# A decoder block on one Trainium2 core: the first projection pair in a written order on three engines, with x loaded ahead of the weights

## The chip, the cores and the metric

One core of one Trainium2 chip. The metric is device time in microseconds (us) of one execution; the kernel before has a median of 2082.65 us in three runs (2078.64 to 2083.49).

## What is computed

A decoder layer on 512 tokens of width 2048, all in float32. The reference, cut to what matters:

```python
h = rms_norm(x, norm1_g)
proj = h @ w_in                       # 2048 x 6160, split into eight parts
qa, ka, va, ra, ga, qb, kb, vb = split(proj)
log_g = log_sigmoid(ga @ gla_gate_w2 + gla_gate_b) / 16
out_a = gla_mixer(qa, ka, va, ra, log_g, gla_onorm_g)      # 4 heads, chunks of 64
out_b = dilated_mixer(norm(qb), norm(kb), vb, rel_bias)    # 8 heads
x = x + concat(out_a, out_b) @ w_out
h2 = rms_norm(x, norm2_g)
x = x + (silu(h2 @ w_gate) * (h2 @ w_up)) @ w_down
```

## The kernel before

**Pairs.** Every matrix product is done in pairs of 512 output columns (`pair`, L183 to L284). One pair multiplies 512 tokens by two neighbouring blocks of 512 columns, by a scheme of the Strassen-Winograd kind: seven products (P1 to P7) of sums of quarters in place of eight plain ones. In the pairs of the projection a product is a sum over four groups g, so a pair has 7 x 4 = 28 steps. A step takes one weight tile of 256 x 512 (called a, b, c or d by its quarter, or a difference of two of these, formed on VectorE at L238, L241, L246 or L251), and splits it into a high part, cast to the short TensorE format on ACT (`wh`, L253), and a low part, the remainder, on VectorE (`wl`, L255). Then TensorE does 12 matmuls of 128 x 128 by 128 x 512 (L263): eight with the high part and four with the low part. The token side is split in the same way beforehand (`Operand.split`, L129 on ACT and L130 on VectorE): operands A11, A12, A22 and the sums S1 to S4, seven for each group, each 128 x 512 in both parts.

**The first pair** (columns 0 to 1023, giving qa and ka) begins with nothing in memory. x has to be loaded, transposed on TensorE block by block (`x_turn`, L422: four transposes of 128 x 128 into one PSUM bank), and scaled by the norm's gain on the way out of PSUM (L429 on VectorE, or L434 on ACT in two halves). The squares of x are summed on ACT (`x_norm`, L407), and four small POOL operations (L411, L113, L114, L415) turn a sum into the row scale `rs1`, which is applied when an accumulator is copied out: the "seed" (L201, ACT), which a later product completes in "close" (L213, VectorE).

**Order.** The program is written as a pair's steps with `step()` between them, which takes the next pieces from a list `background`; `startup()` is the first of them and prepares the operands. A scheduler then orders the instructions on each engine by its own costs. Loads are all issued by SP, in order; at most eight are in flight, and load n waits for load n - 8. `LOADS` gives their order at the start: the gains of the norms, then x in eight pieces of 128 rows x 1024 columns (512 KB) mixed with the weight tiles.

**The gates.** The second pair's steps carry the work of `gates()`: 64 matmuls of 128 x 256 (`ranks`, L505) multiply the operands A11, A12, A22 and S1 by the 16 columns of w_in for the gate, whose small load is `gaw` (L375; tile k), rearranged by three POOL operations (L515 to L517) and split into `gs` (L524, L525). Then come the gate matmuls and the attention heads, in the steps of this pair and the next ones.

**Memory around it.** PSUM has four accumulator buffers (`acc`) and four banks (`bank`). `wh` and `wl` have two buffers each, the weight tiles twelve.

Of the kernel before, what the change touches and what calls it, by code (L numbers as in the profile page):

```python
# [18 lines left out]
P = 128  # L19
# [43 lines left out]
def block_kernel(ctx: ExitStack, tc: tile.TileContext, ins, out):  # L63
# [15 lines left out]

    uid = [0]  # L80

    def nm(s):
        uid[0] += 1
        return f"{s}_{uid[0]}"
# [19 lines left out]
    load(mats, ins["mats"])  # L104
# [74 lines left out]
    def pair(op, rows, w1, w2, final, step, seed_scale=None, pre=()):  # L179
# [3 lines left out]
        q = dict(pre)  # L183
# [102 lines left out]

    background = []
# [68 lines left out]
    def g1_load():  # L356
        load(grow[:, 0, :], ins["norm1_g"].rearrange("(k p) -> k p", p=P))
        load(grow[:, 1, :], ins["norm2_g"].rearrange("(k p) -> k p", p=P))
# [7 lines left out]
    def x_load(t, c):  # L366
        xt[t, c] = apool.tile([P, 1024], F32, name=nm("x"), tag="A")
        load(xt[t, c], x[t * P : (t + 1) * P, c * 1024 : (c + 1) * 1024])
# [30 lines left out]
    ss1 = const([P, 8], "ss1")  # L399
# [3 lines left out]
    raw = {}  # L403

    def x_norm(t):
        for c in range(2):
            tc.keep_in_program_order(nc.scalar.activation(  # L407
                work("L", bufs=2).bitcast(mybir.dt.bfloat16), xt[t, c], AF.Square,
                accum_out=ss1[:, 2 * t + c : 2 * t + c + 1],
            ))  # L410
        nc.gpsimd.tensor_tensor(  # L411
            rs1[:, t : t + 1], ss1[:, 2 * t : 2 * t + 1], ss1[:, 2 * t + 1 : 2 * t + 2], op=ALU.add
        )
        rsqrt_mean(rs1[:, t : t + 1], rs1[:, t : t + 1], D)
        nc.gpsimd.tensor_scalar(nrs1[:, t : t + 1], rs1[:, t : t + 1], -1.0, None, op0=ALU.mult)  # L415

    def x_turn(h, b):
        bk = bank().rearrange("p (j n) -> p j n", j=2)
        for jj in range(2):
            k = 2 * b + jj  # L420
            for m in range(2):
                nc.tensor.transpose(  # L422
                    bk[:, jj, m * P : (m + 1) * P],
                    xt[2 * h + m, k // 8][:, (k % 8) * P : (k % 8 + 1) * P],
                    ident,
                )
        dst = raw[b, h]
        if h == 0 and (b // 2 + b) % 2 == 0:
# [12 lines left out]
    builders = []  # L441
    pre = {}
    for what in LOADS.split():
        if what[0] == "x":
            x_load(int(what[1]), int(what[2]))
        elif what == "g":
            g1_load()
        else:
            pre[what[0], int(what[1])] = load_quarter(
                rows_in, what[0], int(what[1]), col({"a": 0, "b": 512, "d": 512}[what[0]])  # L450
            )

    def first_half(g):
# [7 lines left out]
        x_turn(0, 2 * g)  # L461
        t, b = 2 * g, 2 * g + 1
        builders.append(opx.build(g, raw[t, 0], raw[t, 1], raw[b, 0], raw[b, 1]))
        next(builders[g])

    for g in range(4):
        first_half(g)
    ls_d = [dram([P, 512], f"ls_d{t}") for t in range(4)]

    def startup():  # L470
        small_loads()
        for b in range(8):
            x_turn(1, b)
            yield
        for g, b in enumerate(builders):
            next(b)
            next(b)
            x_norm(g)
            yield
        for b in range(1, 8, 2):  # L480
            x_turn(0, b)
            yield
        for _ in range(2):
            for b in builders:
                next(b)
                yield
        for b in builders:
            yield from b

    def gates():  # L490
        gp = bank()

        def ranks(half):


            parts = (("A22", 2), ("S1", 0)) if half else (("A11", 0), ("A12", 1))
            dst = gp[:, half * 256 : half * 256 + 256]
            n = 0
            for name, kind in parts:
                for g in range(4):  # L500
                    a = opx.t[name, g]
                    for jj in range(2):
                        i = 8 * kind + 2 * g + jj
                        for hl in range(2):
                            nc.tensor.matmul(  # L505
                                dst,
                                gsplit[i // 12][:, i % 12 * 32 : i % 12 * 32 + P],
                                a[:, jj, hl, :],
                                start=(n == 0), stop=(n == 31),
                            )  # L510
                            n += 1
# [7 lines left out]
        gsplit = [mp.tile([P, 512], F32R, name=nm("gs"), tag=t, bufs=1) for t in ("q", "qT")]  # L519
        for i, t in enumerate(gsplit):  # L520
# [6 lines left out]
            )  # L527
        w2 = work("PT")
# [4 lines left out]
        yield  # L533
        ranks(1)
        yield
        ranks(0)
        yield
        ga = work("k", (32, 512))
        nc.scalar.copy(ga, gp[:32, :])
# [7 lines left out]
        )  # L547
        yield
# [687 lines left out]
```

## Time and profile before

| | |
|---|---|
| median of 3 runs | 2082.65 us (2078.64 to 2083.49) |
| profiled execution, time | 2082.12 us |
| its span, first to last instruction | 2079.9 us |
| TensorE busy | 2034.0 us, 98% |
| VectorE busy | 1664.6 us, 80% |
| ACT busy | 1103.5 us, 53% |
| granted TensorE clock, mean | 0.995 |
| moved by DMA | 358.30 MB, 172 GB/s |

In the profile PE is TensorE's matmul queue, PEld its weight loads, DVE VectorE, POOL GpSimd, SP the queue that issues the DMAs. Lines such as L263 are lines of the kernel before. In the timeline the columns are start, duration, engine, line, operation, output <- inputs with the shape, and in brackets the idle time of the engine before it and what ended it. In the waits they are: who waited, for whom, total us, times, longest. PE's duration of one matmul contains the way through the array; matmuls follow each other faster than that.

### The profile page before, as it was taken

Reading aid. Unit: us, or ns where it says so; the run is one execution under the profiler, and the core shown is the slowest. Engines: PE = TensorE matmul, PEld = TensorE weight load, DVE = VectorE, ACT = ScalarE, POOL = GpSimd, SP = SyncE. Lnnn points to the kernel's source line nnn. Section 1 sums busy time; section 2 is a strip of 40 time slices with the busy share of each in tenths; the row PEclk is TensorE's granted clock in tenths of the full one; section 3 lists DMA queues with packets and bytes.
Section 4 is the critical chain, followed back from the end, with each engine's and each line's share of the span. In section 5 each row is a group of like instructions: output and inputs, shape, how many; then the busy total and the mean of one; then the engine's idle time right before and its main releaser. Section 6 shows DMA issues by size and latency. Waiting matters only on the chain.

```text
span 2079.9 us, 25964 instructions
## 1 busy us (share of the span) xinstructions
PE 2034.0 (98%) x9290; PEld 1664.3 (80%) x9290; DVE 1664.6 (80%) x1849; ACT 1103.5 (53%) x1582; POOL 72.0 (3%) x108
## 2 busy tenths in 40 slices
PE   6899999999998999999999999999999999999999
PEld 4688777788876787888888888888888888888887
DVE  5976778677789888878778778778779989979977
ACT  5644455456676676445445445445446645545443
POOL 1100121002000000000000000000000000000000
PEclk9999999999999999999999999999999999999999
DMA  6334572736474866544544543543545855845762
GB/s 221 107 111 159 183 213 76 222 92 208 127 253 139 267 221 195 176 152 133 171 152 133 165 153 129 164 153 129 164 152 156 290 173 186 308 158 181 244 202 72
DMA packets 232683, 358.30 MB, mean 172 GB/s; under 512 B 18039, under 2 KB 92352, under 8 KB 232553
## 3 DMA queue, kind: packets, MB, share of 16 engines
q1 hardware_dynamic: 232552, 356.64, 53.7%
q8 instruction: 73, 1.20, 0.2%
q14 instruction: 58, 0.47, 0.1%
HBM read 294.43 MB, written 64.51 MB: 173 GB/s over the span
## 4 chain that ended last, share of the span: by engine, by line
PE 88%; DMA 4%; DVE 4%; ACT 1%; issue 1%; SPq 1%; POOL 0%; DVEq 0%; ACTq 0%
PE acc L263 82%; PE bank L830 1%; DVE wl L255 1%; PE bank L715 1%; PE bank L737 1%; DVE AS L130 1%; DMA k<-y_d 1%; DMA x<-in_x 1%; ACT wh L253 1%; DMA xn_d<-oT 0%; PE bank L730 0%; PE bank L656 0%; PE bank L638 0%; DMA r<-xn_d 0%; PE bank L505 0%
## 5 line engine op out<-in xcount | busy, mean ns | idle before, releaser
L263 PE MATMUL acc<-wh,AS 128*128 128x512 f32 x3136 | 789.0, 393 | 14.8 <-ACT AS L129 10.6
L263 PEld LDWEIGHTS acc<-wh,AS 128*128 128x128 f32 x3136 | 587.0, 189 | 147.3 <-ACT AS L129 12.7
L253 ACT CAST wh<-wa 128x1024 fp32r<-128x1024 f32 x392 | 412.4, 1054 | 456.6 <-PE acc L263 413.2
L263 PE MATMUL acc<-wh,AA 128*128 128x512 f32 x2352 | 590.2, 393 | 1.2 <-ACT wh L253 1.2
L255 DVE TENSOR_TENSOR wl<-wa,wh 128x1024 fp32r<-128x1024 f32 x392 | 478.1, 1221 | 128.9 <-ACT wh L253 123.1
L263 PEld LDWEIGHTS acc<-wh,AA 128*128 128x128 f32 x2352 | 439.2, 189 | 93.9 <-ACT wh L253 2.1
L263 PE MATMUL acc<-wl,AS 128*128 128x512 f32 x1568 | 421.8, 391 | 4.0 <-DVE wl L255 3.9
L263 PEld LDWEIGHTS acc<-wl,AS 128*128 128x128 f32 x1568 | 294.9, 188 | 67.9 <-DVE wl L255 6.3
L263 PE MATMUL acc<-wl,AA 128*128 128x512 f32 x1176 | 315.3, 390 | 1.0 <-DVE wl L255 1.0
L263 PEld LDWEIGHTS acc<-wl,AA 128*128 128x128 f32 x1176 | 220.4, 188 | 48.4 <-DVE wl L255 2.6
L253 ACT CAST wh<-wb 128x1024 fp32r<-128x1024 f32 x98 | 103.2, 1053 | 137.3 <-PE acc L263 132.2
L253 ACT CAST wh<-wc 128x1024 fp32r<-128x1024 f32 x98 | 103.1, 1053 | 131.7 <-PE acc L263 123.4
L253 ACT CAST wh<-wd 128x1024 fp32r<-128x1024 f32 x98 | 103.3, 1054 | 114.0 <-PE acc L263 103.4
L255 DVE TENSOR_TENSOR wl<-wc,wh 128x1024 fp32r<-128x1024 f32 x98 | 119.6, 1222 | 54.3 <-ACT wh L253 53.9
L255 DVE TENSOR_TENSOR wl<-wd,wh 128x1024 fp32r<-128x1024 f32 x98 | 119.6, 1222 | 54.1 <-ACT wh L253 54.0
L251 DVE TENSOR_TENSOR wa<-wc,wa 128x1024 f32<-128x1024 f32 x98 | 119.6, 1223 | 38.4 <-DMA wc<-in_w_gate 23.0
L255 DVE TENSOR_TENSOR wl<-wb,wh 128x1024 fp32r<-128x1024 f32 x98 | 119.3, 1220 | 12.1 <-ACT wh L253 12.0
L246 DVE TENSOR_TENSOR wb<-wd,wb 128x1024 f32<-128x1024 f32 x98 | 119.6, 1221 | 0.5
L241 DVE TENSOR_TENSOR wa<-wd,wa 128x1024 f32<-128x1024 f32 x98 | 118.9, 1220 | 0.2
L238 DVE TENSOR_TENSOR wa<-wb,wa 128x1024 f32<-128x1024 f32 x98 | 118.3, 1221 | 0.8
L213 DVE SCALAR_TENSOR_TENSOR seed<-acc,rs,seed 128x512 f32<-128x512 f32 x102 | 76.2, 747 | 32.2 <-PE acc L263 32.2
L201 ACT ACTIVATE seed<-acc,rs 128x512 f32<-128x512 f32 x102 | 64.9, 680 | 6.5 <-POOL rs L114 5.6
(249 smaller groups left out, 1154.0 us busy)
## 6 DMA issues: line engine op xcount, KB each, us to landing
wa<-in_w_gate SPq DMA_DIRECT2D x44, 512.0 KB, 4.3
wb<-in_w_up SPq DMA_DIRECT2D x44, 512.0 KB, 4.4
wd<-in_w_up SPq DMA_DIRECT2D x44, 512.0 KB, 4.4
wc<-in_w_gate SPq DMA_DIRECT2D x44, 512.0 KB, 3.5
wa<-in_w_in SPq DMA_DIRECT2D x24, 512.0 KB, 4.5
wb<-in_w_in SPq DMA_DIRECT2D x24, 512.0 KB, 4.8
wd<-in_w_in SPq DMA_DIRECT2D x24, 512.0 KB, 5.7
wc<-in_w_in SPq DMA_DIRECT2D x24, 512.0 KB, 4.0
```

The source lines that it names most:

```text
L130: nc.vector.tensor_tensor(a[:, :, 1, :], src, a[:, :, 0, :].bitcast(F32), op=ALU.subtract)
L201: nc.scalar.activation(t, src[m], AF.Copy, scale=seed_scale(half, m))
L213: nc.vector.scalar_tensor_tensor(seed[m], src[m], seed_scale(half, m), seed[m], op0=ALU.mult, op1=ALU.add)
L238: tt(src, quarter("b", g), src, op=ALU.subtract)
L241: tt(src, quarter("d", g), src, op=ALU.subtract)
L246: tt(src, quarter("d", g), src, op=ALU.subtract)
L251: tt(src, quarter("c", g), src, op=ALU.subtract)
L253: recent["act"] = nc.scalar.copy(wh, src).ins
L255: tt(wl, src, wh.bitcast(F32), op=ALU.subtract)
L263: nc.tensor.matmul(dst[m], a[:, jj, hl, m * P : (m + 1) * P], w[:, jj, :], start=fresh and first, stop=last, skip_group_check=not fresh,)
L715: nc.tensor.matmul(lp[:, :n], qh[:, b * P : (b + 1) * P], kh[:, :n], start=True, stop=True)
L737: nc.tensor.matmul(op, vh[:, k, :], lgs[b][:, k * P : (k + 1) * P], start=(k == 0), stop=(k == b))
```

## The change

The first pair gets a function of its own, `first_pair`, and its instructions on TensorE, VectorE and ACT are issued in the order in which they are written (`manual_schedule`), instead of by the scheduler. That order is a table, `FIRST`, which was found by a search over the queues: entry k + 2 lists what is done at step k between the high and the low matmuls. `t.u4` transposes block 4 of the upper 256 rows (l: lower) and takes it out of PSUM, on VectorE for those named in `ON_VECTOR`, else on ACT; `A11.2` splits that operand for group 2; `+S1.1` forms a sum on VectorE; `sq.2.1` squares a piece of x for rows 256 to 383; `gprep` rearranges the gate's weights; `gate.0` and `gate.1` are the two halves of the gate ranks; `seeda` and `closea` copy and complete an accumulator.

The loads come in another order and size: x in 16 pieces of 256 rows x 256 columns (256 KB, rows of 1 KB), most of them ahead of the weights; the two gains and the identity go through ACT's DMA queue; the rest of `mats`, and with it `gaw` and the other small loads, stand behind all 28 loads on SP.

The products are taken in the order P1, P2, P5, P6, P3, P7, P4 in place of P1, P5, P6, P3, P7, P2, P4; P2 accumulates in two of the banks and P4 in an accumulator of its own. In a step the next weight tile's high part, the difference for the tile after it and the next low part are issued ahead of the step's matmuls. The 64 gate-rank matmuls move from the second pair into step 11 of the first. The second pair is issued behind the first pair's last instructions on ACT, VectorE and TensorE.

The diff, cut to its core:

```diff
-LOADS = "g x00 x10 a0 a1 x01 x11 a2 x20 x30 a3 x21 x31 b0"
+LOADS = (
+    "u4 l3 u2 u0 l5 u1 l2 u3 a0 l1 a1 l0 u6 u7 "
+    "a2 a3 l6 u5 l4 l7 c0 b2 c1 c2 b0 c3 b1 b3"
+)
 PRODUCTS = ("P1", "P5", "P6", "P3", "P7", "P2", "P4")
+UPPER_FIRST = ("P1", "P2", "P5", "P6", "P3", "P7", "P4")
...
+FIRST = (
+    "sq.2.1 t.u4 t.l3 t.u2 A11.2 A22.1 t.u0 t.l5 A11.1 A11.0 t.u1 t.l2",
+    "t.u3 +S1.1 A12.1 t.l1",
+    "A12.0 t.l0 t.u6 S1.1 +S1.0 +S2.1",
+    "A22.0 S1.0 A11.3",
+    "+S3.1 +S2.0 S2.1 t.u7 t.u5 sq.1.3",
+    "t.l4 +S1.2 A12.2",
+    "A12.3 +S4.1",
+    "S1.2",
+    "gprep t.l6 S2.0 t.l7",
+    "sq.3.3 +S1.3 sq.0.3",
+    "sq.0.1",
+    "sq.1.2 S1.3 +S3.0 +S2.3 sq.0.2 +S4.0",
+    "A22.2 sq.1.0 sq.3.1 sq.1.1 A22.3 S4.1 +S2.2",
+    "sq.3.2 sq.2.0 sq.0.0 gate.0 gate.1 S3.0 +S3.3 seeda",
+    "S2.3 sq.3.0 S2.2 +S4.3",
+    "sq.2.2 S4.0 sq.2.3 +S3.2",
+    "+S4.2 seedb",
+    "closea S3.2 S4.2",
+    "",
+    "S3.1 S4.3",
+    "S3.3",
+    "seedc",
+    "",
+    "",
+    "closec",
+    "",
+    "",
+    "",
+    "",
+    "seedd closeb",
+)
+ON_VECTOR = "l0 l2 l3 l5 u2 u3 u4".split()
...
-    load(mats, ins["mats"])
...
+    def first_pair(op, rows, w1, w2, final, unit, pre):
+        tt = nc.vector.tensor_tensor
+        q = dict(pre)
+        items = [(prod, g) for prod in UPPER_FIRST for g in range(op.groups)]
+        sources, high, low = {}, {}, {}
+
+        def fetch(name, g):
+            q[name, g] = load_quarter(rows, name, g, w1 if name in "ac" else w2)
+
+        def total(k):
+            prod, g = items[k]
+            if prod in ("P1", "P2", "P3"):
+                sources[k] = q.pop(("c", g)) if prod == "P2" else q["a" if prod == "P1" else "d", g]
+                return
+            one, two = {"P5": "ba", "P6": "da", "P7": "db", "P4": "ca"}[prod]
+            sources[k] = q[two, g]
+            tt(sources[k], q[one, g], sources[k], op=ALU.subtract)
+            if prod == "P7":
+                fetch("c", g)
+
+        def first_part(k):
+            high[k] = hpool.tile([P, 2, 512], F32R, name=nm("wh"), tag="wh")
+            recent["act"] = nc.scalar.copy(high[k], sources[k]).ins
+
+        def second_part(k):
+            low[k] = hpool.tile([P, 2, 512], F32R, name=nm("wl"), tag="wl")
+            recent["dve"] = tt(
+                low[k], sources.pop(k), high[k].bitcast(F32), op=ALU.subtract
+            ).ins
+            if items[k][0] == "P2":
+                fetch("d", items[k][1])
...
+        def seed(name):
+            prod, half = {"a": ("P1", 0), "b": ("P5", 1), "c": ("P1", 0), "d": ("P1", 1)}[name]
+            seeds[name] = []
+            for m in range(2):
+                t = cpool.tile([P, 512], F32, name=nm("seed"), tag="C")
+                recent["act"] = nc.scalar.activation(
+                    t, dst[prod][m], AF.Copy, scale=row_scale(half, m)
+                ).ins
+                seeds[name].append(t)
+
+        def close(name):
+            prod, half, which = {
+                "a": ("P2", 0, 0), "c": ("P5", 0, 1), "b": ("P1", 1, 1), "d": ("P4", 1, 0)
+            }[name]
+            for m in range(2):
+                recent["dve"] = nc.vector.scalar_tensor_tensor(
+                    seeds[name][m], dst[prod][m], row_scale(half, m), seeds[name][m],
+                    op0=ALU.mult, op1=ALU.add,
+                ).ins
+            final(half, which, seeds[name], None)
...
+        total(0)
+        tokens(0)
+        first_part(0)
+        tokens(1)
+        second_part(0)
+        Y, X = accs(), accs()
+        dst = {"P1": X, "P5": Y, "P6": X, "P3": Y, "P7": X}
+        last = len(items) - 1
+        for k, (prod, g) in enumerate(items):
+            if k == 0:
+                total(1)
+            if k < last:
+                first_part(k + 1)
+            if k + 2 <= last:
+                total(k + 2)
+            if k < last:
+                second_part(k + 1)
+            if g == 0 and prod == "P2":
+                dst["P2"] = [bank(), bank()]
+            elif g == 0 and prod == "P4":
+                dst["P4"] = accs()
+            multiply(k, high[k], (0, 1))
+            tokens(k + 2)
+            multiply(k, low[k], (0,))
+        later(1, lambda: close("d"), hold=True)
...
+    nc.scalar.dma_start(grow[:, 0, :], ins["norm1_g"].rearrange("(k p) -> k p", p=P))
+    nc.scalar.dma_start(mats[:, 0, :], ins["mats"][:, 0, :])
+    nc.scalar.dma_start(grow[:, 1, :], ins["norm2_g"].rearrange("(k p) -> k p", p=P))
...
+    def x_load(h, b):
+        if (h, b // 2) not in xt:
+            xt[h, b // 2] = apool.tile([P, 2, 2, 256], F32, name=nm("x"), tag="A")
+        load(
+            xt[h, b // 2][:, b % 2],
+            x[256 * h : 256 * h + 256, 256 * b : 256 * b + 256].rearrange("(m p) c -> p m c", p=P),
+        )
...
     def small_loads():
+        load(mats[:, 1:, :], ins["mats"][:, 1:, :])
         load(gaw, w_in[:, 3072:3088].rearrange("(k p) n -> p k n", p=P))
...
+    def x_square(t, g):
+        nc.scalar.activation(
+            work("L", bufs=2).bitcast(mybir.dt.bfloat16)[:, :512].rearrange(
+                "p (b c) -> p b c", b=2),
+            xt[t // 2, g][:, :, t % 2, :], AF.Square, accum_out=ss1[:, t, g : g + 1],
+        )
+        squared[t] += 1
...
-    background.append(startup())
-    pace = [5, 4, 4, 4, 3, 2, 2, 2, 1, 1, 1, 1, 2, 2, 2, 2]
-    pair(opx, rows_in, col(0), col(512), final_proj("qa", "ka"), paced(pace), row_scale, pre=pre)
-    background.extend([gates(), bias_tables()])
+    with tc.manual_schedule(engines=ordered):
+        gains()
+        first_pair(opx, rows_in, col(0), col(512), final_proj("qa", "ka"), first_unit, pre)
     opm = Operand(4)
-    pair(opx, rows_in, col(1536), col(1024), final_proj("va1", "va0"), rate((22, 1), (6, 0.6)), row_scale)
+    with ExitStack() as behind:
+        for engine in ("act", "dve", "pe"):
+            behind.enter_context(tc.issue_after(recent[engine]))
+        background.extend([gates(), bias_tables()])
+        pair(opx, rows_in, col(1536), col(1024), final_proj("va1", "va0"), rate((22, 1), (6, 0.6)), row_scale)
     flow = rate((50, 0.6), (34, 0.5))
     pair(opx, rows_in, col(3088), col(4112), final_proj("qb0", "kb0"), flow, row_scale)
     pair(opx, rows_in, col(5648), col(5136), final_proj("vb1", "vb0"), flow, row_scale)
```

`first_unit` maps a token to the function that does it. The step that turns the last square's sum into the row scale has one more POOL addition, since there are four partial sums now.

More of the change, by code (lines that the diff above doesn't have):

```diff
@@ L440, in block_kernel @@
     rows_in = [(512 * g, 512 * g + 256) for g in range(4)]
[L441 removed]
     pre = {}
     for what in LOADS.split():
[L444 to L447, printed above, removed]
[L448 to L453 removed]
+        name, i = what[0], int(what[1])
+        if name in "ul":
+            x_load("ul".index(name), i)
+        else:
+            pre[name, i] = load_quarter(rows_in, name, i, col(512 if name == "b" else 0))
+    small_loads()
+    for g in range(4):
         for b in (2 * g, 2 * g + 1):
@@ L490, in gates @@
[L490 to L511, printed above, removed]
+    ls_d = [dram([P, 512], f"ls_d{t}") for t in range(4)]
@@ new lines, in first_unit @@
+    def first_unit(what, *args):
+        if what == "t":
+            x_turn("ul".index(args[0][0]), int(args[0][1]), args[0] in ON_VECTOR)
+            return
+        args = [int(a) for a in args]
+        if what == "sq":
+            x_square(*args)
+            return
+        if what == "gprep":
+            rank_weights()
+            return
+        if what == "gate":
+            ranks(*args)
+            return
+        (g,) = args
+        r11, r21, r12, r22 = raw[2 * g, 0], raw[2 * g, 1], raw[2 * g + 1, 0], raw[2 * g + 1, 1]
+        tt = nc.vector.tensor_tensor
+        if what == "+S1":
+            tt(r21, r21, r22, op=ALU.add)
+        elif what == "+S2":
+            tt(r21, r21, r11, op=ALU.subtract)
+        elif what == "+S3":
+            tt(r11, r22, r21, op=ALU.subtract)
+        elif what == "+S4":
+            tt(r21, r12, r21, op=ALU.subtract)
+        else:
+            opx.split(what, g, {"A11": r11, "A12": r12, "A22": r22, "S3": r11}.get(what, r21))
@@ L518, in gates @@
         kf = kinds.rearrange("p a g j n -> p (a g j) n")
-        gsplit = [mp.tile([P, 512], F32R, name=nm("gs"), tag=t, bufs=1) for t in ("q", "qT")]
+        gsplit = rank["w"] = [
+            mp.tile([P, 512], F32R, name=nm("gs"), tag=t, bufs=1) for t in ("q", "qT")
+        ]
         for i, t in enumerate(gsplit):
@@ L527, in gates, with ranks @@
             )
+        rank["p"] = bank()
+    def ranks(half):
+        parts = (("A22", 2), ("S1", 0)) if half else (("A11", 0), ("A12", 1))
+        dst = rank["p"][:, half * 256 : half * 256 + 256]
+        n = 0
+        for name, kind in parts:
+            for g in range(4):
+                a = opx.t[name, g]
+                for jj in range(2):
+                    i = 8 * kind + 2 * g + jj
+                    for hl in range(2):
+                        nc.tensor.matmul(
+                            dst, rank["w"][i // 12][:, i % 12 * 32 : i % 12 * 32 + P],
+                            a[:, jj, hl, :], start=(n == 0), stop=(n == 31),
+                        )
+                        n += 1
+    def gates():
         w2 = work("PT")
```

96 lines of the change are left out of this document (42 added, 54 removed).

## The prediction

> **What bounds the kernel now.** I read the page's busy shares and slices first, then the windows, the waits and the timeline of the first 230 us.
>
> ```profile
> PE 2034.0 (98%) x9290; PEld 1664.3 (80%) x9290; DVE 1664.6 (80%) x1849; ACT 1103.5 (53%) x1582; POOL 72.0 (3%) x108
> ...
> PE   6899999999998999999999999999999999999999
> ```
>
> TensorE is the bound, and what it loses it loses at the left edge: a slice is 52 us, the first has 6 tenths and the second 8. The windows (busy us of each engine, then granted clock, DMA share, GB/s):
>
> ```profile
> 0.00:10.00 10.00, 2.74 (x10) 1.79 (x10) 0.35 (x2) 1.79 (x2) 0.77 (x9) 1.00 0.71 229
> 10.00:20.00 10.00, 4.78 (x18) 3.26 (x18) 3.05 (x3) 3.66 (x8) 0.00 (x0) 1.00 1.03 408
> 20.00:40.00 20.00, 19.61 (x100) 16.03 (x98) 16.88 (x22) 16.50 (x36) 4.59 (x7) 1.00 0.82 257
> 40.00:60.00 20.00, 11.14 (x25) 7.63 (x26) 13.05 (x17) 12.39 (x20) 7.17 (x10) 0.67 0.00 0
> 60.00:75.00 15.00, 11.01 (x45) 8.14 (x46) 15.00 (x22) 12.63 (x22) 3.23 (x4) 0.99 0.00 1
> 75.00:123.00 48.00, 48.00 (x212) 39.74 (x213) 40.12 (x42) 22.51 (x26) 0.00 (x0) 1.00 0.69 208
> ```
>
> Until 20 us PE waits for data; from 40 to 75 it waits for its operands, with the granted clock down to 0.67 as well; from 75 it never waits. The waits name the causes, and the timeline the places:
>
> ```profile
> PE acc L263 <- ACT AS L129: 9.2, 2, 5.7
> PE bank L422 <- DMA x<-in_x: 8.6, 6, 3.4
> ACT wh L253 <- DMA wa<-in_w_in: 8.3, 2, 7.5
> ACT seed L201 <- POOL rs L114: 5.6, 2, 3.6
> ```
> ```profile
> 20.15 1.22 PE L263 MATMUL acc<-wh,AA 128*128 128x512 f32 x2
> ...
> 38.00 4.13 POOL L114 TENSOR_TENSOR rs<-rs,mhalf 128x1 f32<-128x1 f32 x1
> ...
> 42.16 0.69 ACT L201 ACTIVATE seed<-acc,rs 128x512 f32<-128x512 f32 x1 [3.56 <-POOL rs L114]
> ...
> 45.30 3.78 PE L263 MATMUL acc<-wh,AS 128*128 128x512 f32 x8 [5.69 <-ACT AS L129]
> ...
> 122.14 1.98 PE L263 MATMUL acc<-wh,AA 128*128 128x512 f32 x8
> ```
>
> The first product starts at 20.15. On ACT the seed waits for a POOL power of 4.13 us with the next operand casts queued behind it, and PE stands 5.69 us. At 122.14 product 337 starts: the second pair.
>
> PE's useful work up to there: products follow each other every 0.2267 us in the calm stretch, so 336 of them are 76.2 us; 64 transposes at 0.109 us (clock up) are 7.0. So 122.1 - 83.2 = 38.9 us are lost. That is all the change can win. Compared instruction by instruction, the five queues hold the same order in both kernels from the middle of the second pair on (PE's 884th matrix instruction, about 228 us), and the same number of PE instructions before it. So only waits and clock before that point count.
>
> **The change, part by part.** The common mark is the start of the second pair with the 64 gate-rank matmuls done. Before, these stand inside the second pair: two blocks of 3.79 us, so the mark is 122.1 + 7.6 = 129.7.
>
> *Arrival of x.* SP issues x first (0.7 us instead of 2.1), and 256 KB pieces. The first instruction of ACT that is not a DMA issue is now the square sq.2.1, which reads l2 and l3; l2 is the seventh piece. Everything on ACT stands behind it: the operand casts A11.2 and A22.1, u0's evacuation, and so PE's banks and first weights. By l2, 7 x 256 + 80 KB = 1872 KB have to land. Before, 1744 KB had landed when the first weight tile did (9.47 us) and 2256 KB at the second (11.32), which gives 9.9. In the trace's DMA records a 1 KB packet takes 46 ns in the median and a 4 KB packet 159, so 1 KB rows are 16% slower per byte; I take 10.2 (9.3 if the earlier issue counts in full, 12.5 if 1 KB rows from x cost half as much again).
>
> *First product.* From there ACT runs: square (8 squares of 1024 follow each other in about 1.05 with their read; half of it 0.59), four 512 casts at 0.51, two evacuations of two halves at 0.36, one 1024 cast of 1.05: 0.59 + 2.04 + 1.44 + 1.05 = 5.1 us. First product: **15.4** instead of 20.15 (14.4 to 17.6).
>
> *PE's content from 15.4.* 336 products at 0.2295, their spacing at 24 to 39 us where transposes and casts run beside them: 77.1. Seven of the 16 blocks are still to be turned, 28 transposes at 0.109: 3.1. The ranks: 7.6. Together 87.8.
>
> *Clock.* Before, the first 8 products took 2.7 us instead of 1.8 and their transposes 0.213 us instead of 0.109; the clock came up at 22.8. The granted-clock records change in steps of 3.41 us, so I charge one step at half speed: 1.7 (0 to 3.4, two steps, as in the dips at 43 and 53 us). The Trainium skill, "TensorE: Matmul & The Clock Gate", says in Part 1 that the first 3.4 us of activity run at half clock, and in Part 4 that transposes do not count as busy in the same way: by that rule the turning from 5 to 12 us warms nothing, and the term would be the 3.4. Before, the transposes from 17.8 on all ran at 0.213, which fits it.
>
> *VectorE as bound.* 28 low parts and 16 weight subtractions at 1.135 (start to start) are 49.9; 28 operand low parts, 16 sums and 7 evacuations at 0.60 are 30.7; six closes at 0.66 and the gate weights 4.5: 85 us. From 6.6 us with some 5 of waiting it ends near 97, before PE. ACT has some 64 us. I followed the three written queues step by step with these prices: the low part is ready before PE asks for it, at every step. Cost 0; if that cover failed, each 1.14 us operation too late is 1.14 us of PE.
>
> *Gate weights.* Their load (gaw) moves behind all 28 loads on SP. By the rows 10.4 MB precede it: after l2, 9 pieces at 0.74, 12 weight tiles at 1.34, the rest of mats 0.4 and gaw itself 2.2 (2048 packets of 64 B at 11 ns over 16 engines, and 0.8 to be seen) give 35.5 us. Then POOL's three steps (0.29 + 1.29 + 0.46), ACT's two gs casts, four evacuations, one operand cast and the weight cast of step 8, which is queued behind them: 3.8. That cast is ready at 41.4; PE reaches step 8 at 15.4 + 22.0 + 3.1 + 1.7 = 42.2. Cost 0, with 0.8 us to spare; each further us of delay is one of PE (0 to 4).
>
> *Squares and scales.* The POOL power is paid before the first seeds, while PE does the 7.6 us of ranks in step 11; ACT waits some 3 us there, and the casts behind it are wanted only after step 12. Cost 0; without that cover up to the 5.7 of before. The other moves on SP cost nothing: tri and stri are first read at 198 us, and the d weights, behind the tiny gq load whose issue held SP 7.59 us before, land at 40 to 45 and are first read near 50.
>
> *Sum.* 15.4 + 87.8 + 1.7 = **104.9** against 129.7: 24.8 less. In the second pair the gate chain starts differently: before had waits of 0.3, 0.3 and 0.9 us there; I add 1.0 (0 to 2.5). Net -23.8. The profiled execution took 2082.12 us (span 2079.9 and 2.2 around it): 2058.3; the median of the runs, 2082.65, is 0.5 above it, so I forecast **2058.8**.
>
> **Rivals.**
>
> *Gate weights late (0.20).* Loads 10 to 15% slower than reckoned put gaw at 38 to 40 us; the spare 0.8 is gone, PE stands 2 to 4 us at step 8 and may drop its clock for one step (1.7). About 2063, up to 2067. For it: 229 GB/s in the first window. Against: 408 in the second.
>
> *Cold longer (0.10).* Two clock steps: 2060.5. For it: both dips of the first 75 us lasted 6.8 us, and the skill's rule on transposes, above.
>
> *More than reckoned (0.04).* l2 lands near 9 and the clock comes up with the transposes: 2056.
>
> *Slower (0.04).* The start becomes bound by the transfers. Step 8's cast comes 5.9 us after gaw; to eat 24 us it has to come at 66, gaw at 60: 10.7 MB at under 183 GB/s. Then 2083 and more; at 160 GB/s gaw lands at 69 us: 2091. For it: 16 half-size transfers of 1 KB rows at 8 KB pitch, which no load of before has. Against: 2 KB rows at that pitch (w_out, w_down) keep 84 ns a packet, and 1 KB stretches elsewhere move 340 GB/s. The Trainium skill, "DMA: Bandwidth & Descriptors", Bandwidth, asks for at least 1 MiB per DMA and has 138 GB/s at 64 KB and 341 at 1 MB. An estimate between them, 240 GB/s, would put x's end 6 us later and the result near 2064; the trace's 408 GB/s with 512 KB transfers speaks against taking single-transfer rates for a full queue.
>
> *Given back (0.03).* The first pair shortens, but the second waits for weights or the gate chain instead: within 0.3% (6 us, about what a measurement can tell from no change). Against: wa's buffers come free in the difference product, some 16 us before they are wanted.
>
> **How the numbers follow.** The forecast holds 0.59: 2056 to 2061. The range takes in the cold and late rivals: 2054.5 to 2067. Faster by over 0.3% is all but the last two: 0.93; same 0.03; slower 0.04.
>
> **What would show it.** First product at 14.4 to 17.6, ACT's first square ended by the DMA of x; PE without waits over 1 us from 20 us on except at step 8 and its rank block in the middle of the pair; the first product of the second pair near 105; clock at 1.00 from 22 us. Wrong: PE waits for low parts (L355) in many steps, the second pair past 110, or waits after 230 us that before had not.

## The result and the profile after

The changed kernel takes 2062.78 us in the median of 4 runs (2060.72 to 2063.0), the kernel before 2083.07 beside it; the ratio is 0.9903, with a 95% interval of 0.9884 to 0.9921. The forecast of 2058.8 was 4.0 us too low. The profiled execution took 2060.72 us (span 2058.9), 21.4 less than that of before.

The page's busy shares and the slices of TensorE:

```profile
PE 2030.1 (99%) x9290; PEld 1666.1 (81%) x9290; DVE 1666.0 (81%) x1854; ACT 1101.9 (54%) x1592; POOL 74.9 (4%) x112
...
PE   8999999999999999999999999999999999999999
```

The left edge has closed: the first slice of 51 us went from 6 tenths to 8, the second from 8 to 9, with the same 9290 matrix instructions. The windows of the changed kernel from 10 us on (from:to, length, busy us of each engine, clock, DMA share, GB/s):

```profile
10.00:20.00 10.00, 8.56 (x40) 6.81 (x39) 9.05 (x13) 8.15 (x18) 0.00 (x0) 0.83 1.01 347
20.00:40.00 20.00, 20.00 (x100) 16.70 (x99) 17.36 (x23) 14.99 (x29) 2.00 (x4) 1.00 0.82 264
40.00:60.00 20.00, 19.70 (x118) 17.29 (x117) 19.80 (x23) 14.91 (x34) 8.92 (x2) 1.00 0.36 123
60.00:75.00 15.00, 11.95 (x41) 9.26 (x40) 8.46 (x11) 10.36 (x18) 9.10 (x19) 0.77 0.00 0
```

From 10 to 20 us TensorE is busy for 8.56 us (4.78 before), and from 20 to 60 it is filled (before it had 11.1 of 20 us between 40 and 60). One hole is left: between 60 and 75 it has 11.95 of 15 us and a clock of 0.77. VectorE, too, falls to 8.46 there after 19.80 of 20 in the window ahead of it. The hole's place in the timeline of the changed kernel (start, length, engine and line, tiles, and in brackets the wait ahead and who ended it):

```profile
14.57 3.61 PE L371 MATMUL acc<-wh,AA 128*128 128x512 f32 x8
41.70 2.11 PE L371 MATMUL acc<-wh,AS 128*128 128x512 f32 x8 [0.30 <-ACT wh L351]
51.00 8.86 POOL L569 TENSOR_TENSOR ss<-ss 128x2 f32<-128x2 f32 x1 [12.30 <-ACT L L562]
58.59 1.22 DVE L345 TENSOR_TENSOR wa<-wd,wa 128x1024 f32<-128x1024 f32 x1
60.49 0.58 POOL L154 TENSOR_TENSOR rs<-rs,mhalf 128x1 f32<-128x1 f32 x1
62.76 1.26 ACT L385 ACTIVATE seed<-acc,rs 128x512 f32<-128x512 f32 x2 [7.50 <-POOL rs L154]
63.50 3.78 PE L371 MATMUL acc<-wh,AS 128*128 128x512 f32 x8 [3.05 <-ACT seed L385]
64.99 1.23 DVE L355 TENSOR_TENSOR wl<-wa,wh 128x1024 fp32r<-128x1024 f32 x1 [5.18 <-ACT wh L351]
```

Read upwards from 63.50: TensorE stands 3.05 us at step 12 for ScalarE's first seed; the seed has waited 7.50 us for GpSimd's power; and the power, a matter of 0.58 us, stands behind an add of two numbers per partition that took 8.86 us. The same add of the next chain, at 61.33, takes 0.19 us. The long one ends at 51.00 + 8.86 = 59.86. VectorE's row without a pause ends at 58.59 + 1.22 = 59.81. VectorE stops there because its next operation, at 64.99, needs a weight cast that stands on ScalarE behind the seed, and so behind the power itself: the add came through only when VectorE had run out of work.

In before, the 4.13 us that I had taken for the price of a power end at 42.13, and this is VectorE's last row ahead of its pause there (timeline of before):

```profile
41.01 0.69 DVE L149 TENSOR_TENSOR xT<-xT 128x512 f32<-128x512 f32 x1
```

This operation ends at 41.70; 42.13 is 0.43 later, about the 0.05 of the changed kernel and the 0.38 by which an undisturbed power (0.57) is longer than an add (0.19).

### The profile page after: what moved, and what is told of

Same layout as the page of the kernel before. It is cut to its first block, busy times and chain, and to the rows that moved or that the text cites. A ratio compares the mean times of both kernels' runs of the same rounds, so it can differ in the third digit from the quotient of the medians.

```text
span 2058.9 us, 26021 instructions
## 1 busy us (share of the span) xinstructions
PE 2030.1 (99%) x9290; PEld 1666.1 (81%) x9290; DVE 1666.0 (81%) x1854; ACT 1101.9 (54%) x1592; POOL 74.9 (4%) x112
## 4 chain that ended last, share of the span: by engine, by line
PE 90%; DMA 4%; DVE 3%; ACT 1%; issue 1%; POOL 1%; SPq 0%; DVEq 0%; ACTq 0%
PE acc L303 82%; PE acc L371 2%; PE bank L984 1%; PE bank L869 1%; DVE wl L295 1%; PE bank L891 1%; DMA x<-in_x 1%; DMA xn_d<-oT 1%; DMA k<-in_w_in 0%; PE bank L792 0%; PE bank L810 0%; PE bank L884 0%; POOL ss L569 0%; DMA top<-mix_d 0%; DMA wb<-in_w_in 0%
## 5 line engine op out<-in xcount | busy, mean ns | idle before, releaser
L303 PE MATMUL acc<-wh,AS 128*128 128x512 f32 x3008 | 753.6, 392 | 3.1 <-ACT wh L293 1.7
L303 PEld LDWEIGHTS acc<-wh,AS 128*128 128x128 f32 x3008 | 562.3, 188 | 127.0 <-issue 3.3
L293 ACT CAST wh<-wa 128x1024 fp32r<-128x1024 f32 x376 | 396.0, 1054 | 436.7 <-PE acc L303 395.7
L303 PE MATMUL acc<-wh,AA 128*128 128x512 f32 x2256 | 564.4, 392 | 0.0
L295 DVE TENSOR_TENSOR wl<-wa,wh 128x1024 fp32r<-128x1024 f32 x376 | 457.7, 1218 | 103.0 <-ACT wh L293 97.6
L303 PEld LDWEIGHTS acc<-wh,AA 128*128 128x128 f32 x2256 | 421.0, 188 | 89.2 <-issue 2.3
L303 PE MATMUL acc<-wl,AS 128*128 128x512 f32 x1504 | 403.4, 390 | 0.5 <-DVE wl L295 0.5
L303 PEld LDWEIGHTS acc<-wl,AS 128*128 128x128 f32 x1504 | 282.3, 188 | 60.7 <-DVE wl L295 1.8
L303 PE MATMUL acc<-wl,AA 128*128 128x512 f32 x1128 | 302.9, 390 | 1.9 <-DVE wl L295 1.9
L303 PEld LDWEIGHTS acc<-wl,AA 128*128 128x128 f32 x1128 | 211.9, 188 | 47.5 <-DVE wl L295 3.4
```

The source lines that it names most:

```text
L293: recent["act"] = nc.scalar.copy(wh, src).ins
L295: tt(wl, src, wh.bitcast(F32), op=ALU.subtract)
L303: nc.tensor.matmul(dst[m], a[:, jj, hl, m * P : (m + 1) * P], w[:, jj, :], start=fresh and first, stop=last, skip_group_check=not fresh,)
```

## The experiments

**What is in dispute.** Theory L (a lock): the add, which reads SBUF, is kept out for as long as VectorE goes from one operation with two SBUF inputs to the next without a pause. Theory F (first use): GpSimd pays for its first operation of a kind, or for its first after a long idle time. All changes below are to the changed kernel.

**after_again**: no edit.

> The changed kernel once more. In its first profile GpSimd's first add of the norm chain (128x2) took 8.86 us, from 51.00 to 59.86, and it ended 0.05 us after VectorE's last operation in an unbroken row (59.81). Theory L (lock): the add reads SBUF and is kept out while VectorE issues operations with two SBUF inputs without a pause. It comes again: 8 to 9.5 us, ended within 0.2 us of VectorE's next pause; 2060 to 2064 us. Theory F (first use): what costs is the first operation of the chain after 12 us of idle GpSimd, so 8 to 9 us again, but not tied to VectorE's pause. Theory R (chance): another length, anywhere from 0.2 to 9 us, and the time with it, 2055 to 2063.

Measured: 2063.56 us (ratio 0.9906, 0.9892 to 0.9921). The add took 8.86 us once more, from 49.90 to 58.76, and VectorE's last operation of its row ended at 58.71. It is no chance. TensorE again waited 3.05 us, and the second pair began at 108.05 instead of 109.90: in this run the clock came up at 11.03 us and held until the hole, where it lost one step of 3.41 us instead of two.

**warm**: the three kinds of operation once on a scratch tile, at the program's start.

```diff
+    warm = const([P, 4], "warm")
+    nc.gpsimd.memset(warm, 1.0)
+    nc.gpsimd.tensor_tensor(warm[:, :2], warm[:, :2], warm[:, 2:], op=ALU.add)
+    nc.gpsimd.tensor_scalar(warm[:, :1], warm[:, :1], 0.5, 1.0, op0=ALU.mult, op1=ALU.add)
+    nc.gpsimd.tensor_tensor(warm[:, :1], warm[:, :1], mhalf[:, :1], op=ALU.pow)
```

> The chain's three kinds of GpSimd operation (add 128x2, scale, power) are done once on a small tile of their own at the start of the program. F: the add of the chain then takes about 0.2 us, ScalarE's wait at the first seed falls from 7.5 to under 1 us, the second pair starts near 104.5 and the time is 2055 to 2058. L: nothing changes at 51 us, the add takes 8 to 9.5 us again, second pair near 110, 2060 to 2064.

Timeline of warm, GpSimd:

```profile
1.07 0.19 POOL L153 TENSOR_TENSOR warm<-warm 128x2 f32<-128x2 f32 x1
...
49.99 8.87 POOL L574 TENSOR_TENSOR ss<-ss 128x2 f32<-128x2 f32 x1 [12.22 <-ACT L L567]
```

The very first add of the program takes 0.19 us, the later one 8.87 all the same; 2064.16 us (0.9907, 0.9891 to 0.9924). Paying for the kind of operation early changes nothing: that half of F is out. An idle time of 12 us is still possible.

**dvewait**: VectorE is made to pause, by a copy of the chain's result behind the first two chains.

```diff
+    seen = const([P, 2], "seen")
...
+            if t < 2:
+                nc.vector.tensor_copy(seen[:, t : t + 1], nrs1[:, t : t + 1])
```

> Behind the chains of the first two row blocks VectorE copies the result of the chain (128x1), so it stands there until GpSimd has done it: VectorE's unbroken row is broken at about 53.3 us. L: the add ends within 0.2 us of VectorE reaching the copy, some 2.4 us instead of 8.9; the chain ends 1.3 us later, near 54.7; ScalarE's wait at the seeds is under 2 us, PE's wait at step 12 under 0.5 us, the clock stays at 1.00, second pair at 104 to 106, 2055 to 2059 us. F: the add takes 8.9 us all the same, VectorE stands 7 us at the copy and the low parts behind it are late: PE waits as long as before or longer, 2062 to 2070.

Timeline of dvewait, rows of VectorE, GpSimd and TensorE:

```profile
49.63 2.45 POOL L570 TENSOR_TENSOR ss<-ss 128x2 f32<-128x2 f32 x1 [12.30 <-ACT L L563]
51.33 0.69 DVE L171 TENSOR_TENSOR AA<-xT,AA 128x512 fp32r<-128x512 f32 x1
53.62 0.15 DVE L575 COPY seen<-nrs 128x1 f32<-128x1 f32 x1 [1.60 <-POOL nrs L573]
...
59.46 8.99 POOL L570 TENSOR_TENSOR ss<-ss 128x2 f32<-128x2 f32 x1 [2.67 <-ACT L L563]
...
73.58 2.76 PE L372 MATMUL acc<-wh,AS 128*128 128x512 f32 x8 [3.62 <-ACT wh L352]
```

VectorE's operation ends at 52.02 and, the copy being next, nothing follows; the add, begun at 49.63, ends at 52.08. A VectorE that stops sets GpSimd free after 2.45 us instead of 8.86, with the same 12.3 us of idle GpSimd ahead of it: idle time has no fixed price either. TensorE's wait at step 12 is gone. But the time is 2061.1 us (0.99, 0.9882 to 0.9919) and the second pair began at 107.97, not the 2055 to 2059 us and 104 to 106 expected: the third chain, which has no copy behind it, was now kept out for 8.99 us, and TensorE stood 3.62 us four steps later, its weight cast queued behind the seed of that chain. The wait had moved on to the next chain.

**dvewait4**: the same copy behind all four chains (the line without its condition).

> As dvewait, with VectorE's copy behind all four chains instead of two. In dvewait the second pair began at 107.97, with one PE wait of 3.62 us at 73.58 (the third chain's add had taken 8.99 us there) and one half-clock step (some 1.7 us). L: each of the first adds of a chain ends within 0.2 us of VectorE reaching the copy, none takes over 3 us, that wait and the clock step go: second pair at 102 to 104.5, waits over 1 us between 20 and 100 us gone, 2056 to 2059 us. Rival D (another wait behind it): PE stands at the same step for another reason, second pair at 106 to 109, 2060 to 2063.

Timeline of dvewait4, GpSimd, and its window from 60 to 75:

```profile
50.04 2.45 POOL L570 TENSOR_TENSOR ss<-ss 128x2 f32<-128x2 f32 x1 [12.30 <-ACT L L563]
...
59.89 2.58 POOL L570 TENSOR_TENSOR ss<-ss 128x2 f32<-128x2 f32 x1 [2.67 <-ACT L L563]
```
```profile
60.00:75.00 15.00, 14.10 (x62) 11.29 (x61) 13.24 (x19) 10.22 (x17) 7.28 (x10) 1.00 0.10 34
```

No add takes over 2.6 us, TensorE has 14.10 of the 15 us and the clock stays at 1.00. The second pair begins at 104.13, the time is 2056.89 us (0.9881, 0.9864 to 0.9897). sq21 below, which ran beside it and keeps the hole, took 2062.37, and none of the runs of one lies in the range of the other. Four tiny copies that make VectorE *wait* win 5 to 6 us. (By the ratios to before, 0.9881 against 0.9903 and 0.9906, it is nearer 5.)

**actnorm**: the chains without GpSimd, on ScalarE.

```diff
+    eps = const([P, 1], "eps")
+    nc.gpsimd.memset(eps, EPS)
...
-            nc.gpsimd.tensor_tensor(ss1[:, t, :2], ss1[:, t, :2], ss1[:, t, 2:], op=ALU.add)
-            nc.gpsimd.tensor_tensor(rs1[:, t : t + 1], ss1[:, t, :1], ss1[:, t, 1:2], op=ALU.add)
-            rsqrt_mean(rs1[:, t : t + 1], rs1[:, t : t + 1], D)
-            nc.gpsimd.tensor_scalar(nrs1[:, t : t + 1], rs1[:, t : t + 1], -1.0, None, op0=ALU.mult)
+            r = rs1[:, t : t + 1]
+            nc.scalar.activation(ss1[:, t, :], ss1[:, t, :], AF.Copy, accum_out=r)
+            nc.scalar.activation(r, r, AF.Ln, scale=1.0 / D, bias=eps)
+            nc.scalar.activation(r, r, AF.Exp, scale=-0.5)
+            nc.scalar.activation(nrs1[:, t : t + 1], r, AF.Copy, scale=-1.0)
```

> The four chains are done on ScalarE (sum of the four parts, Ln, Exp of minus a half of it, negative), so no GpSimd operation stands before the seeds. L: ScalarE's waits at the seeds go, at four times about 1 us of ScalarE; second pair at 102 to 105, 2056 to 2059 us. Rival S: the added ScalarE time makes the operand casts late instead, PE waits 1 us and more at steps 10 to 14, second pair at 106 to 109, 2060 to 2063.

Measured: 2055.81 us (0.9877, 0.9862 to 0.9892), second pair at 103.21. No add on GpSimd is left to be kept out, and the hole is gone. A chain takes ScalarE 1.1 us (55.30 to 56.40), less than the 4.0 us from the first add to the end of the last scaling in dvewait4 (50.04 to 54.00). The window and the one wait that is left in the pair:

```profile
60.00:75.00 15.00, 15.00 (x68) 12.43 (x67) 14.52 (x18) 12.73 (x29) 0.00 (x0) 1.00 0.10 36
```
```profile
41.10 1.20 PE L373 MATMUL acc<-wh,AS 128*128 128x512 f32 x4 [1.23 <-ACT wh L353]
```

**probe**: what does an add see in a row of adds? 80 of them at the start of GpSimd's queue.

```diff
+    probe = const([P, 4], "probe")
+    nc.gpsimd.memset(probe, 1.0)
+    for _ in range(80):
+        nc.gpsimd.tensor_tensor(probe[:, :2], probe[:, :2], probe[:, 2:], op=ALU.add)
```

> 80 adds of 128x2 on a small tile of their own, one behind the other, are put on GpSimd at the start, ahead of the gate weights' three steps; 0.28 us each undisturbed. L: those before VectorE's first two-input work (about 8 us) and beside evacuations from PSUM take 0.2 to 0.3 us; beside two-input work in an unbroken row they are stretched to the next start of a VectorE operation or to its next pause, some of them by several us, so the 80 last well past 24 us. F: the first takes several us, all others 0.2 to 0.3, and the row ends near 30 us. The gate weights may come late in this kernel and with them step 8 of TensorE, so its time says little: 2060 to 2090.

GpSimd's timeline in two windows, and the chain's add after them:

```profile
6.40 4.00 POOL L154 TENSOR_TENSOR probe<-probe 128x2 f32<-128x2 f32 x15
```
```profile
20.21 17.16 POOL L154 TENSOR_TENSOR probe<-probe 128x2 f32<-128x2 f32 x23
```
```profile
57.92 7.71 POOL L573 TENSOR_TENSOR ss<-ss 128x2 f32<-128x2 f32 x1 [13.50 <-ACT L L566]
```

Beside evacuations of PSUM, 15 adds take 4.00 us, 0.27 each with the step between them. Beside VectorE's two-input work, 23 take 17.16 us, 0.75 each: most are 0.52 or 1.06 long and end just after the next VectorE operation has begun. So L was right that this work holds GpSimd off, but in part only: standing in an unbroken row itself, GpSimd got a turn at every such start, and none of the 80 was kept out for longer than 1.06 us. The chain's add, after 13.5 us of idle time, was kept out for 7.71 us. (The row of adds lasted to 43 us and delayed the gate weights; the single run of 2068.59 says little.)

**busy**: so GpSimd is kept at work between the gate weights and the chain.

```diff
+        busy = const([P, 4], "busy")
+        nc.gpsimd.tensor_copy(busy, gaw[:, 0, :4])
+        for _ in range(16):
+            nc.gpsimd.tensor_tensor(busy[:, :2], busy[:, :2], busy[:, 2:], op=ALU.add)
```

> Behind the gate weights' steps on GpSimd (from about 38 us) stand 16 small adds of their own, so that GpSimd is at work without a pause until about 50 us, where the first chain begins; in probe adds in an unbroken row were let in at every start of a VectorE operation (0.5 or 1.06 us each). If GpSimd's being idle before decides (it gets its turn only when it already stood in the row): the chain's first add takes 0.5 to 1.2 us, ScalarE's wait at the seeds falls below 3 us, second pair 102.5 to 106, 2056 to 2060. If not: one of the adds (any of the 17) is kept out for several us until VectorE's next pause, second pair 107 to 111, 2060 to 2065.

```profile
38.06 11.02 POOL L656 TENSOR_TENSOR busy<-busy 128x2 f32<-128x2 f32 x14
49.50 0.72 POOL L569 TENSOR_TENSOR ss<-ss 128x2 f32<-128x2 f32 x1 [0.42 <-ACT L L562]
```

The chain's first add takes 0.72 us, the chain goes on in turns, the second pair begins at 104.07, and the one run took 2055.99 us. Sixteen useless adds on an engine that is 4% busy are worth as much as the copies. What sets the turns is not settled: in this kernel the third chain's add was let in after 0.69 us, 2.68 us idle; in dvewait the same add, 2.67 us idle, was kept out for 8.99. Idle time by itself does not decide. Nor does it decide that VectorE's row had begun while GpSimd asked for nothing, as the third chain of before shows (its timeline):

```profile
51.56 1.23 DVE L255 TENSOR_TENSOR wl<-wa,wh 128x1024 fp32r<-128x1024 f32 x1 [2.11 <-ACT wh L253]
56.22 0.70 POOL L411 TENSOR_TENSOR rs<-ss 128x1 f32<-128x1 f32 x1 [6.03 <-ACT L L407]
```

From 51.56 on VectorE goes without a pause; GpSimd, idle for 6.03 us, asks at 56.22 and is let in at the next start. And work just ahead of it does not protect an operation either: the power of before that took 4.13 us stood 0.08 us behind two others of its chain.

**sq21**: the first square leaves the head of ScalarE's queue.

```diff
-    "sq.2.1 t.u4 t.l3 t.u2 A11.2 A22.1 t.u0 t.l5 A11.1 A11.0 t.u1 t.l2",
+    "t.u4 t.l3 t.u2 A11.2 A22.1 t.u0 t.l5 A11.1 A11.0 t.u1 t.l2",
...
-    "+S3.1 +S2.0 S2.1 t.u7 t.u5 sq.1.3",
+    "+S3.1 +S2.0 S2.1 t.u7 t.u5 sq.1.3 sq.2.1",
```

> The square sq.2.1, the first work of ScalarE's queue, which waits for the seventh piece of x (7.3 us of waiting), is moved to the fourth step; nothing else changes. If ScalarE standing behind that piece holds the first product: it starts at 12.5 to 13.5 instead of 14.2 to 15.0, and the time falls by 1 to 2 us, 2060 to 2062. If the x pieces themselves and the turning are the limit: first product 14.0 to 15.0 as before, 2061 to 2064. The 3 us wait at step 12 and the long GpSimd add stay in both.

Measured: 2062.37 us (0.9908, 0.9893 to 0.9923), first product at 14.41. No gain. Timelines of ScalarE and TensorE in sq21:

```profile
11.91 1.06 ACT L351 CAST wh<-wa 128x1024 fp32r<-128x1024 f32 x1
```
```profile
14.03 0.63 PE L578 MATMUL bank<-mats,x 128*128 128x128 f32 x4 [2.89 <-DMA x<-in_x]
14.41 1.85 PE L371 MATMUL acc<-wh,AA 128*128 128x512 f32 x7
```

ScalarE is ready 1.5 us earlier (its weight cast ends at 12.97 instead of 14.52), but TensorE's ninth turning, that of l1, stands ahead of the first product in its queue and waits for its piece of x. l1 is the tenth load, behind the weight tile a0. In the changed kernel the two limits coincide: there, too, the turning waited for x until 13.94, and it ended at 14.57, where the cast had ended at 14.52.

**x8**: x in 8 transfers of 512 KB.

```diff
-    "u4 l3 u2 u0 l5 u1 l2 u3 a0 l1 a1 l0 u6 u7 "
-    "a2 a3 l6 u5 l4 l7 c0 b2 c1 c2 b0 c3 b1 b3"
+    "u4 l3 u2 u0 l5 a0 l1 a1 u6 "
+    "a2 a3 l6 c0 b2 c1 c2 b0 c3 b1 b3"
...
+            x[256 * h : 256 * h + 256, 512 * g : 512 * g + 512].rearrange("(m p) c -> p m c", p=P),
```

> The changed kernel with x in 8 transfers of 512 KB (256 rows of 2 KB) instead of 16 of 256 KB, in the order in which the first halves came; the order on the engines stays. The first product needs five of the eight (2.6 MB), where it now needs nine of the sixteen; the first square needs the second instead of the seventh. Theory S (the small pieces make the early start): the first product starts at 15.5 to 17 instead of 14.2 to 15.0, and the time rises by 1 to 3 us, 2063 to 2067. Theory N (size of the pieces doesn't matter; turning and casting set the start): 14.2 to 15.2, 2061 to 2064.

Measured: 2062.65 us (0.9909, 0.9894 to 0.9924), first product at 14.46, though the first square starts at 6.37 instead of 9.33. Here, too, TensorE's ninth turning waits for its x, until 13.42, but what ends last is ScalarE's weight cast, at 14.41: TensorE waits 0.41 us for it. The size of the pieces brings nothing that this measurement can tell, nor do the 1 KB rows cost anything that it can tell.

**planner**: the loads and program order of the change, the queues left to the planner.

```diff
-    with tc.manual_schedule(engines=ordered):
+    with ExitStack():
```

> The changed kernel without the fixed order on the three engines: the same loads and the same program order, but the planner sets the queues. TensorE's queue is then nearly the same; ScalarE's has the first two weight casts ahead of the operand casts and of two evacuations, and the first rank weights elsewhere. Theory O (the order on ScalarE and VectorE brings the gain): first product at 16 to 18, waits of several us in the first 75 us, second pair at 114 to 125, 2066 to 2080. Theory X (the early x pieces bring it): first product 14 to 15.5, second pair 106 to 111, 2060 to 2065.

Timelines of VectorE, TensorE and, later, GpSimd:

```profile
16.96 1.23 DVE L355 TENSOR_TENSOR wl<-wa,wh 128x1024 fp32r<-128x1024 f32 x1 [2.40 <-ACT wh L351]
18.10 1.88 DVE L585 TENSOR_TENSOR xT<-bank,g 128x512 f32<-128x512 f32 x3
```
```profile
18.84 4.16 PE L578 MATMUL bank<-mats,x 128*128 128x128 f32 x20 [9.62 <-DVE xT L585]
22.76 2.08 PE L371 MATMUL acc<-wh,AA 128*128 128x512 f32 x8
```
```profile
35.73 5.27 POOL L650 COPY v<-k 128x128 f32<-128x128 f32 x1 [29.12 <-DMA k<-in_w_in]
```

The planner puts the first two weight casts, and on VectorE their low parts, ahead of the evacuations. The casts wait for a0 and a1 (2.58 us ahead of the second cast), the evacuations for the low parts, and TensorE's next transposes stand 9.62 us for a bank. The first product comes at 22.76, 8 us later than with the fixed order and later than O expected. Yet the second pair begins at 112.85, only 2.95 us behind the changed kernel and earlier than O expected: in this order no GpSimd operation of the chains takes over 1.5 us, and TensorE is busy without a gap from 60 to 75 us. Here it is the first copy of the gate weights that VectorE keeps out: 5.27 us, over its six next operations, and it ends 0.15 us behind the last of them. The time is 2067.67 us (0.993, 0.9915 to 0.9945). So some 14 of the 20 us come from the loads, the order of the products and the earlier ranks together, which were not tried apart; the written queues add 5 (x8, beside it, took 2062.65), and 11 where the hole is gone (best, beside it, 2056.84).

**rankslate**: the gate weights and the 64 rank matmuls back in the second pair.

```diff
-    "gprep t.l6 S2.0 t.l7",
+    "t.l6 S2.0 t.l7",
...
-    "sq.3.2 sq.2.0 sq.0.0 gate.0 gate.1 S3.0 +S3.3 seeda",
+    "sq.3.2 sq.2.0 sq.0.0 S3.0 +S3.3 seeda",
...
     def gates():
+        rank_weights()
...
+        ranks(1)
+        yield
+        ranks(0)
```

> The changed kernel with the gate weights' preparation and the 64 rank matmuls back in the second pair. They stand between step 11's first part and step 12, where the long GpSimd add falls. L: the add ends with VectorE's pause as before, so the first pair ends no earlier; TensorE waits 9 to 11 us at step 12 instead of 3.05, the second pair starts at 107 to 112 (with one or two clock steps), the 7.6 us of ranks come on top in the second pair: 2068 to 2073. Rival: the ranks only move, the wait stays near 3 us and the second pair starts 7 us earlier, 2060 to 2064.

```profile
62.06 3.71 PE L371 MATMUL acc<-wh,AS 128*128 128x512 f32 x8 [9.46 <-ACT seed L385]
```

The wait at step 12 is 9.46 us instead of 3.05: the 7.6 us of ranks were indeed its cover. The clock went to half within it, for 10.2 us, the second pair began at 107.70 with the ranks still to come, and the time is 2069.28 us (0.9932, 0.9916 to 0.9949; its runs lie between 2064.8 and 2075.26, and the profile is of the slowest).

**best**: actnorm with the gate weights' preparation one step later (*gprep* at the head of entry 9 instead of 8).

> actnorm with the gate weights' preparation one step later (entry 9 instead of 8), so that step 8's weight cast is not queued behind the two gs casts, which wait for GpSimd 3.2 us there. In actnorm PE stood 1.23 us at step 8 and the second pair began at 103.21. If the casts are all that was late: no wait over 0.5 us at steps 8 and 9, second pair at 101.7 to 102.8, 2053 to 2056 us. If it only moves the wait to step 9 or 10: second pair 103 to 104, 2055 to 2057.

The wait at step 8 went and the second pair began at 101.58 (101.7 to 102.8 expected). The time, expected at 2053 to 2056, did not follow: 2056.84 us (0.9879, 0.9865 to 0.9894), not to be told from actnorm's 2055.81. From the second pair's middle, where the order is the same in all, to the last matmul this profile took 1849.6 us and actnorm's 1846.9; over all profiles here that stretch lies between 1845.7 and 1850.8, more than the 1.6 us at stake.

## Why the prediction came out as it did

**Inside the range, in part by luck.** 2062.78 lies in the range of 2054.5 to 2067, but not in the 2056 to 2061 that the forecast itself was to hold. The range reaches so far for late gate weights and a longer cold clock at the start, and neither came; what took their place was a wait that the prediction had put at nothing.

**Right: the bound and the start.** The loss was at the left edge, and the gain came from there: at the mark (second pair begun, ranks done) the changed kernel is at 109.90 against 129.7, 19.8 us earlier. At the 720th product the two differ by 19.8 us still, so the second pair gave nothing back; the 1.0 us that I added for its gate chain was not needed. The remaining 1.5 us to the 21.4 of the profiles lie within the scatter of the later stretch.

**Right in size, half right in reason: the first product.** 14.57 against 15.4 (14.4 to 17.6; 10.2 + 5.1 is 15.3), the first square at 9.33 against 10.2. But sq21 shows that ScalarE standing behind l2 is only one of two limits of nearly equal length; the other, which I left out, is l1's turning on TensorE. It was not tried with l1's load ahead of a0.

**Right: the gate weights.** GpSimd began on them at 36.56 (35.5 reckoned for their landing) and TensorE had a wait of 0.30 us at step 8, at 41.70 (41.4 to 42.2 reckoned). The rival of late gate weights did not come. The rivals of slow transfers and of VectorE as the bound did not either: 347 GB/s from 10 to 20 us, and no wait for a low part in the changed kernel's first pair.

**Right in size by luck: the clock at the start.** The first eight products took 3.61 us instead of 1.98: 1.6 more, about the 1.7 that I charged. The records show another course, though. The granted clock stood at 1.00 from 11.38 to 14.79 us, when TensorE had done nothing but turning since 5.2 (from 11.4 on a transpose followed every 0.109 us instead of 0.213); it fell to half from 14.79 to 18.21, after a wait of 1.41 us for x. In after_again and warm it was up at 11.03 and 9.52 and held until the hole; in sq21 a wait of 2.89 us for x at the same place did not bring it down. The Trainium skill, "TensorE: Matmul & The Clock Gate", Part 4, says that transposes do not count as busy in the same way; here the trace disagrees, for the clock rose on transposes alone, and the rival of two cold steps by that rule fell.

**Wrong: "Squares and scales ... Cost 0".** I took the 4.13 us of before for the length of a GpSimd power, some 3 us of it for ScalarE to wait, all under the 7.6 us of ranks. By the rows above it was no length but a wait for VectorE's next pause, and the change made VectorE's row longer: 8.86 us. The cover was outrun by 3.05 us, and the clock fell for 6.8 us, in which the three groups of products from 63.50 on took 3.78, 1.91 and 2.29 us instead of 1.98, 1.07 and 1.98: 2.95 more. Together 6.0; less the 0.8 of the earlier first product that is 5.2, against the 5.0 by which the mark missed 104.9. These 5.0, less the 1.0 that was not needed, are the 4.0 by which the forecast was low. The clock's part differs from run to run: in sq21 a wait of 3.04 us at the same step cost no clock at all. In dvewait4, actnorm and busy, where the wait is away, the second pair begins at 104.13, 103.21 and 104.07, and the times are 2056 to 2057: about what the sum gives without that wait and with the two corrections, 2058.8 - 1.0 - 0.8 = 2057.0.

The rows could have told. In before, the power's end lies 0.43 us behind VectorE's last operation, and the later powers of before took 0.9 us. The Trainium skill, "SBUF — State Buffer", in the section on the two separate sides, says that VectorE's operations with two SBUF inputs and GpSimd's that read SBUF take an exclusive lock on a shared port pair, held for the whole instruction, with the loser blocked. The trace agrees that the loser is blocked, and goes further: the add was kept out not for one VectorE operation (0.7 or 1.2 us) but for ten more in a row.

## What to carry to other kernels

A long duration in a row is a price only if it comes again under other neighbours: look at what ends with it. Packing one engine fuller can keep another waiting, as VectorE did GpSimd here, and the cure may be a pause, a handful of idle operations, or the small chain on a third engine. And a cover (here the ranks) has to be compared with the wait as it will be after the change, not as it was.

## What was not expected of the hardware

- An add of 128x2 on GpSimd took 0.19 us undisturbed, 0.26 to 1.15 when it took turns with VectorE, and up to 8.99 when VectorE ran ten and more two-input operations without a pause. In all nine profiles with an add of over 2 us it ended 0.05 us after VectorE's last operation.
- Such a row of VectorE's does not always keep GpSimd out: a GpSimd in an unbroken row of adds was let in at every start of an operation (probe, busy), and so was one that had been idle for 6.03 us (before, at 56.22). What decides between turns and none stays open.
- The granted clock rose on transposes alone, at 9.5 to 11.4 us, after they had come one behind the other from about 6 us on. In before, where they came in groups with waits between them, it first rose at 22.8.
